# Modulation rows of a decoder layer: summed over partitions by chains of accumulating DMAs instead of matmuls, with loads and norm factors rearranged around them

## The chip, the cores and the metric

The kernel runs on one core of a Trainium2 chip. The metric is the device time of one execution in microseconds (us), the median of several runs. The core has five engines with an instruction list each: TensorE (PE) multiplies matrices and writes to PSUM; VectorE (DVE) and ScalarE (ACT) compute element by element; GpSimd (POOL) does the same more slowly; SyncE (SP) only issues DMAs. Each engine takes its list in order, and waits for others on semaphores. DMAs are issued by SP, ACT and POOL.

## The reference

One decoder layer on 512 tokens of width 1024 in float32:

```python
mod = silu(c) @ w_ada + b_ada                        # (1, 6 * 1024)
shift1, scale1, gate1, shift2, scale2, gate2 = split(mod, 6)
h = rmsnorm(x, norm1_g) * (1 + scale1) + shift1
qa, ka, va, qd, kd, vd, ga, gd = split(h @ w_in)
out_a = sliding_window_attention(qa, ka, va)         # 8 heads, window 128, sinks, ALiBi
out_d = diff_attention(qd, kd, vd)                   # 4 heads, two softmax maps, per-head rmsnorm
merged = sigmoid(ga) * (out_a @ w_branch_swa) + sigmoid(gd) * (out_d @ w_branch_diff)
x = x + gate1 * (merged @ w_out)
h2 = rmsnorm(x, norm2_g) * (1 + scale2) + shift2
a, g = split(h2 @ w_up)                              # 2 * 2816 columns
x = x + gate2 * ((gelu(causal_conv3(a)) * g) @ w_down)
out = rmsnorm(x, final_g)
```

## The kernel before

Every product is made of three matmuls on values split into a high and a low part (`mm3`, lines 122 to 124; `split`, lines 118 and 119: ScalarE casts the high part, VectorE subtracts it to get the low part). The stages follow each other along PE's list:

- **0 to 62 us**: statistics of x, shift1 and scale1 from `w_ada`, the first projection (L385).
- **62 to 308 us, the attention stage**: one long list that the program writes out by hand for PE (`manual_schedule`, L530). Its steps are the scores, softmaxes, transposes and values of four pairs of sliding-window heads (`swa_*`) and of 16 blocks of differential attention (`diff_*`; 4 heads h, 4 query blocks n each). Between them `fill(n)` puts n ticks of plain projections: a tick is one `k` step of three 512-column matmuls of the current unit. Units (weight columns of w_in, or a branch projection) stand in the list `units`; `prefetch` keeps two of them loaded. Buffers for raw weights come from one ring of four (`raw_tile`, L107).
- **308 to 345 us**: the output projection with `gate1` folded into `w_out` (`load_rows`, L1109), `oc`.
- **345 to 690 us**: the second norm, `w_up` with the convolution (`up`, L1274), then `w_down` (`dc`, L1889) and the final norm. Its weight sums are made by accumulating DMAs on POOL (L1183, L1874).

The order on VectorE, ScalarE, POOL and SP in the attention stage isn't written out: a planner orders ready instructions by priority and its own cost estimates. `high_priority` raises, `issue_after` puts behind a given instruction of the same engine.

**The modulation rows.** shift2, scale2 and both gates (four vectors of 1024, eight half rows of 512) are needed only after attention. The generator `ada_rows` makes them beside it: every `ADA_EVERY` = 8 ticks (L561) it loads 256 rows x 512 columns of `w_ada` (`ada_load`, L839), and VectorE multiplies by silu(c) and adds into `ac`, 128 partitions x 512 (`arow`, L861 and L863). Four loads make one half row, which still has to be summed over the 128 partitions. `ada_spread` does that on PE with a matrix of ones:

```python
    nc.tensor.matmul(
        pr[gs], ones[:, gs], ac[:, g * P : (g + 1) * P], start=True, stop=True, tile_position=(0, 32 * g)
    )
```

ScalarE copies the result out (L885), and POOL stores 2 KB of it to `mod_rows` in DRAM (L886). `flush("row")` or `after(ADA_LAG, ...)` says where in PE's list these matmuls stand.

**Who reads `mod_rows`.** `g1b` (gate1, both halves of row 0, L1077, on POOL) multiplies the rows of w_out; `m2` (rows 1 and 2, L1082) is transposed on PE (`pm`, L1086) for the second norm; `g2b` (row 3) is read by the last stage at 468 us.

**The norm factors of differential attention.** `diff_values(h)` multiplies the probabilities with the values. `stats` (flushed in the third block of the next head) takes the sums of squares, and `rstd_m2` makes the factor: POOL raises to a power (L185), VectorE improves it (L193, L195). `turn_norm` (flushed in the first block of the head after that) spreads the factor by four transposes (`rb`, L818) and scales the output.

Of the kernel before, what the change touches and what calls it, by code (L numbers as in the profile page):

```python
# [14 lines left out]
P = 128  # L15
# [11 lines left out]
WB = 3  # L27
HP = 100000
ST = 6
ADA_LAG = 1  # L30
# [6 lines left out]
STAT_LAG = 10  # L37
NORM_LAG = 16
# [16 lines left out]
def kernel(  # L55
# [50 lines left out]
    def raw_tile(shape, name):  # L106
        return wp.tile(shape, F32, tag="raw", bufs=4, name=name)  # L107
# [422 lines left out]
    man.enter_context(tc.manual_schedule(engines={nc.tensor.engine}))  # L530
    units, loaded, later = [], [], []
# [7 lines left out]
    def fill(n):  # L539
        for _ in range(n):  # L540
            if not current:
                prefetch()
                if loaded:
                    wts, run = loaded.pop(0)
                    current.append(run(wts))
                    if tick[0]:
                        prefetch()
# [16 lines left out]
    beside = {"row": [], "sum": [], "norm": [], "turn": []}  # L564
# [153 lines left out]

    def diff_scores(*ss):
# [20 lines left out]
        for s, sps, w in ops:  # L740
# [3 lines left out]
            for m in range(2):  # L744
                st = ap.tile([P, w], F32, tag="st", bufs=ST, name=f"sd{h}_{n}_{m}")
                with tc.high_priority(offset=HP):
                    nc.vector.tensor_tensor_reduce(
                        st, sps[m], ddf[:, 512 - w : 512], 1.0, -3e38, ALU.add, ALU.max, mx[:, m : m + 1]
                    )
# [39 lines left out]
    def diff_values(h):  # L789
# [14 lines left out]
        def stats():  # L804
# [7 lines left out]
            rstd_m2(rs, r2, NT, P, ap)  # L812
            nc.vector.tensor_mul(rs, rs, r0)
# [29 lines left out]
    def ada_rows():  # L843
        todo = [(idx, hf, k) for idx in range(4) for hf in range(2) for k in range(0, KT, 2)]
        r = ada_load(*todo[0])
        yield
        for (idx, hf, k), job in zip(todo, todo[1:] + [None]):
            nxt = ada_load(*job) if job else None
            if k == 0:
                ac = big.tile([P, S], F32, tag=("sq2", "g2b1")[hf], name=f"arow{idx}{hf}")  # L850
            if idx == 0 and hf == 1 and k in ROW_BEHIND:
                hold = tc.issue_after(pairs[sorted(pairs)[ROW_BEHIND[k]]].divided.ins)
            elif tick[0] > ADA_EASY:
                hold = tc.high_priority(offset=HP // 2)
# [9 lines left out]
            if k == KT - 2:  # L864
                row = lambda idx=idx, hf=hf, ac=ac: ada_spread(idx, hf, ac)
                if group_ahead:
                    beside["row"].append(row)
                else:
                    after(ADA_LAG, row)
            r = nxt  # L870
            yield

    spread = []


    def ada_spread(idx, hf, ac):
        pr = tbank(f"pr{idx}{hf}", (P, P))
        for g in range(4):
            gs = slice(32 * g, 32 * g + 32)
            nc.tensor.matmul(  # L880
                pr[gs], ones[:, gs], ac[:, g * P : (g + 1) * P], start=True, stop=True, tile_position=(0, 32 * g)
            )
        row = big.tile([P, P], F32, tag="g2b0", name=f"row{idx}{hf}")
        with tc.high_priority(offset=HP):
            spread.append(nc.scalar.copy(row, pr))  # L885
        nc.gpsimd.dma_start(  # L886
# [1058 lines left out]
```

## Time and profile before

| | us |
|---|---|
| median of 3 runs (lowest, highest) | 692.67 (692.59, 693.79) |
| the profiled execution | 691.85 |
| its span, first to last instruction | 689.8 |
| PE busy in the span | 680.0 |
| DVE busy | 565.5 |
| ACT busy | 383.7 |
| POOL busy | 82.0 |
| granted TensorE clock | 0.997 |

The page of the profile gives the busy time of each engine, the span in 40 slices, DMA queues, the chain of work that ended last, the costliest groups of instructions, and the DMA issues with their time to landing. Further views list who waited for whom, the timeline of an engine, the instructions of a line or a tile, and busy times by windows. L12 is line 12 of the kernel; a releaser stands behind "<-".

### The profile page before, as it was taken

What the parts mean: (1) busy time and instruction counts of PE and PEld (TensorE: products, weight loads), DVE (VectorE), ACT (ScalarE), POOL (GpSimd) and SP (SyncE); (2) the same over time, 40 slices, a digit from 0 to 9 for tenths busy, and PEclk for the clock granted to TensorE, in tenths of its full rate; (3) what the DMA queues carried; (4) which work ended last, traced back from release to release, by engine and by line L of the source; (5) the groups of instructions that cost most, each with busy time, mean ns of one, the idle gap of its engine ahead of it and who ended that gap; (6) DMA issues with size and microseconds to landing.
All of it is one profiled execution on the core that took longest, in us unless ns stands there. A gap on an engine that the chain in (4) does not pass through costs nothing. (4 is left out here: it accounts for less than half of the span.)

```text
span 689.8 us, 11249 instructions
## 1 busy us (share of the span) xinstructions
PE 680.0 (99%) x4203; PEld 592.7 (86%) x4203; DVE 565.5 (82%) x1073; ACT 383.7 (56%) x686; POOL 82.0 (12%) x100
## 2 busy tenths in 40 slices
PE   8999999999999999999999999999999999999995
PEld 5887777788888888888899999999999999888884
DVE  5898987987885666673689988888888999979997
ACT  7676666546543323332477656655555666656665
POOL 3000000000001100000030101112120002540300
PEclk9999999999999999999999999999999999999998
DMA  9985454552555575239635897777888648997903
GB/s 309 350 237 180 140 158 135 166 166 67 153 153 184 185 226 171 91 113 315 214 65 120 179 212 191 173 165 218 193 229 215 154 155 203 197 197 196 167 1 122
DMA packets 115926, 121.81 MB, mean 177 GB/s; under 512 B 4447, under 2 KB 93344, under 8 KB 115872
## 3 DMA queue, kind: packets, MB, share of 16 engines
q1 hardware_dynamic: 96958, 95.09, 43.9%
q0 software_dynamic: 18720, 25.73, 22.3%
q8 instruction: 33, 0.54, 0.3%
q10 hardware_dynamic: 194, 0.28, 0.1%
q14 instruction: 21, 0.17, 0.1%
HBM read 118.97 MB, written 2.11 MB: 176 GB/s over the span
## 5 line engine op out<-in xcount | busy, mean ns | idle before, releaser
L1274 PE MATMUL up<-t,m_whi 128*128 128x256 f32 x512 | 93.1, 283 | 0.0
L1274 PEld LDWEIGHTS up<-t,m_whi 128*128 128x128 f32 x512 | 79.9, 192 | 0.0
L1274 PE MATMUL up<-t,m_wlo 128*128 128x256 f32 x256 | 72.4, 283 | 0.0
L1274 PE MATMUL up<-bh,p_whi 128*128 128x256 f32 x232 | 65.7, 283 | 0.0
L1274 PE MATMUL up<-bl,p_whi 128*128 128x256 f32 x232 | 65.7, 283 | 0.0
L1274 PE MATMUL up<-bh,p_wlo 128*128 128x256 f32 x232 | 65.7, 283 | 0.0
L863 DVE SCALAR_TENSOR_TENSOR arow<-ra,cs,arow 128x512 f32<-128x512 f32 x56 | 42.0, 749 | 18.9 <-DMA ra<-in_w_ada_dram 18.2
L1274 PEld LDWEIGHTS up<-t,m_wlo 128*128 128x128 f32 x256 | 49.2, 192 | 0.0
L1274 PEld LDWEIGHTS up<-bh,p_whi 128*128 128x128 f32 x232 | 44.5, 192 | 0.0
L1274 PEld LDWEIGHTS up<-bl,p_whi 128*128 128x128 f32 x232 | 44.5, 192 | 0.0
L1274 PEld LDWEIGHTS up<-bh,p_wlo 128*128 128x128 f32 x232 | 44.5, 192 | 0.0
L1183 POOL DMA_DIRECT2D s<-in_w_up_dram x21 | 27.0, 1360 | 138.6 <-DMA s<-in_w_up_dram 69.3
L1211 ACT CAST m_whi<-s 128x1024 fp32r<-128x1024 f32 x31 | 32.5, 1047 | 11.1 <-DVE s L1205 7.7
L1215 DVE TENSOR_TENSOR m_wlo<-s,m_whi 128x1024 fp32r<-128x1024 f32 x31 | 37.8, 1218 | 0.0
L1274 PE MATMUL up<-t,p_whi 128*128 128x256 f32 x176 | 32.2, 283 | 0.0
L886 POOL DMA_DIRECT2D mod_rows<-row x8 | 4.9, 612 | 203.4 <-ACT row L885 203.4
L1274 PEld LDWEIGHTS up<-t,p_whi 128*128 128x128 f32 x176 | 27.5, 192 | 0.0
L1281 ACT ACTIVATE gT<-a,cv 128x512 f32<-128x512 f32 x22 | 17.7, 813 | 16.9 <-DVE a L1316 15.8
L185 POOL TENSOR_TENSOR r<-ms,mhalf 128x1 f32<-128x1 f32 (+1 forms) x16 | 12.7, 792 | 120.7 <-DVE ms L183 73.1
L1211 ACT CAST p_whi<-wa 128x1024 fp32r<-128x1024 f32 x18 | 18.8, 1042 | 12.6 <-PE up L1274 12.6
L1215 DVE TENSOR_TENSOR p_wlo<-wa,p_whi 128x1024 fp32r<-128x1024 f32 x18 | 22.0, 1222 | 3.8 <-ACT p_whi L1211 3.2
L1274 PE MATMUL up<-t,p_wlo 128*128 128x256 f32 x88 | 24.9, 283 | 0.0
(491 smaller groups left out, 2063.2 us busy)
## 6 DMA issues: line engine op xcount, KB each, us to landing
ra<-in_w_ada_dram SPq DMA_DIRECT2D x32, 512.0 KB, 4.1
wa<-in_w_up_dram SPq DMA_DIRECT2D x22, 512.0 KB, 4.1
s<-in_w_up_dram SPq DMA_DIRECT2D x21, 512.0 KB, 4.6
s<-in_w_up_dram POOLq DMA_DIRECT2D x21, 512.0 KB, 7.3
adaw<-in_w_ada_dram SPq DMA_DIRECT2D x12, 512.0 KB, 7.3
w<-in_w_in_dram SPq DMA_DIRECT2D x12, 512.0 KB, 4.5
a<-in_w_up_dram SPq DMA_DIRECT2D x11, 512.0 KB, 4.6
b<-in_w_down_dram SPq DMA_DIRECT2D x10, 512.0 KB, 4.6
```

The lines of the kernel that those rows point to most:

```text
L185: nc.gpsimd.tensor_tensor(r0, ms, mhalf[:, :n], ALU.pow)
L863: nc.vector.scalar_tensor_tensor(ac, r[:, a], cc, ac, ALU.mult, ALU.add)
L886: nc.gpsimd.dma_start(mod_rows[idx, hf * S : (hf + 1) * S].rearrange("(g n) -> g n", g=4), row[0:P:32])
L1183: nc.gpsimd.dma_start(dst, upblock(*blk), accum_op=ALU.add)
L1211: nc.scalar.copy(W[J, name][0], R[J, SRC[name]])
L1215: nc.vector.tensor_sub(lo, R[J, SRC[name]], hi.bitcast(F32))
L1274: nc.tensor.matmul(o[u], w[:, k, cu], b[:, k], start=name in ("p1", "m5", "p2") and k == 0 and x == 0, stop=k == 3 and x == 2, skip_group_ ...
L1281: nc.scalar.activation(grow(j), av[J][:, u], AF.Identity, bias=cv[:, 66 + j : 67 + j], scale=cv[:, 44 + j : 45 + j])
```

## The change

- `ada_spread` is gone. `ada_sum` issues, on POOL, seven DMAs that add the upper half of the remaining partitions of `ac` to the lower half (64, 32, 16, 8, 4, 2, 1 partitions of 2 KB), and one that stores partition 0 to `mod_rows`. It is called as soon as the last multiply of the half row is traced; `ac` takes turns in three buffers instead of two.
- The ring of raw buffers has six instead of four; `ada_rows` loads two jobs ahead instead of one, so each multiply is traced 8 ticks later than before; its high priority is dropped. The scratch for DMA descriptors is set to 8192 bytes.
- All units are listed at the start, and `due` counts how many may run, so that `prefetch` can load across the ends of groups. SP's order in the attention stage is that of the program.
- The norm factor is made in two parts: `stats` starts it (the power on POOL), and `end` finishes it after the row maxima of the next scores, one block later; `turn_norm` stands two ticks into the second block of the head after, instead of in the first. For the last head `end` comes 3 ticks after `stats`.
- The broadcasts of `g1b` and its bias, and two constant parts of `m2`, are issued by SP instead of POOL; the two VectorE instructions on `g1b` stand behind the second merge.

```diff
--- before.py
+++ after.py
@@ -25,9 +25,10 @@
 SWA_PAIRS = 4
 DIFF_HEADS = 4
 WB = 3
+RAW = 6
+ADA_AHEAD = 2
 HP = 100000
 ST = 6
-ADA_LAG = 1
 ADA_EVERY = 8
 ADA_EASY = 20
 
@@ -35,6 +36,7 @@
 ADA_START = 4
 V_LAG = 13
 STAT_LAG = 10
+END_LAG = 3
 NORM_LAG = 16
 SWA_FILL = (2, 2, 5, 2, 2, 2, 2, 3)
 DIFF_FILL = (3, 2, 4, 2)
@@ -104,7 +106,7 @@
         return bank("v", 1, [P, S], name)
 
     def raw_tile(shape, name):
-        return wp.tile(shape, F32, tag="raw", bufs=4, name=name)
+        return wp.tile(shape, F32, tag="raw", bufs=RAW, name=name)
 
     splits = []
 
@@ -527,8 +529,8 @@
             mm3(o[:, sl], wh[:, k], wl[:, k], rh[:, k, sl], rl[:, k, sl], k == 0, k == KT - 1)
 
     man = ExitStack()
-    man.enter_context(tc.manual_schedule(engines={nc.tensor.engine}))
-    units, loaded, later = [], [], []
+    man.enter_context(tc.manual_schedule(engines={nc.tensor.engine, nc.sync.engine}))
+    units, loaded, later, due = [], [], [], [0]
     current, tick = [], [0]
 
     def prefetch():
@@ -540,7 +542,8 @@
         for _ in range(n):
             if not current:
                 prefetch()
-                if loaded:
+                if loaded and due[0]:
+                    due[0] -= 1
                     wts, run = loaded.pop(0)
                     current.append(run(wts))
                     if tick[0]:
@@ -561,7 +564,7 @@
             if tick[0] >= ADA_START and tick[0] % ADA_EVERY == 0:
                 next(ada, None)
 
-    beside = {"row": [], "sum": [], "norm": [], "turn": []}
+    beside = {"sum": [], "end": [], "norm": [], "turn": []}
 
     def after(n, fn):
         later.append([n, fn])
@@ -716,6 +719,8 @@
     AW = 384
 
 
+    maxima = []
+
     def diff_scores(*ss):
         ops = []
         for s in ss:
@@ -744,9 +749,9 @@
             for m in range(2):
                 st = ap.tile([P, w], F32, tag="st", bufs=ST, name=f"sd{h}_{n}_{m}")
                 with tc.high_priority(offset=HP):
-                    nc.vector.tensor_tensor_reduce(
+                    maxima.append(nc.vector.tensor_tensor_reduce(
                         st, sps[m], ddf[:, 512 - w : 512], 1.0, -3e38, ALU.add, ALU.max, mx[:, m : m + 1]
-                    )
+                    ))
                 pm.append(st)
             scored[s] = mx, pm
 
@@ -809,8 +814,16 @@
             nc.vector.reciprocal(r0, sums[h][:, 0])
             nc.vector.tensor_mul(r2, r0, r0)
             nc.vector.tensor_mul(r2, r2, pss)
-            rstd_m2(rs, r2, NT, P, ap)
-            nc.vector.tensor_mul(rs, rs, r0)
+            half = rstd_start(r2, NT, P, ap)
+
+            def end():
+                rstd_end(rs, *half, NT, ap)
+                nc.vector.tensor_mul(rs, rs, r0)
+
+            if h < 3:
+                beside["end"].append(end)
+            else:
+                after(END_LAG, end)
 
             def turn_norm():
                 rb = tbank(f"rb{h}")
@@ -842,16 +855,18 @@
 
     def ada_rows():
         todo = [(idx, hf, k) for idx in range(4) for hf in range(2) for k in range(0, KT, 2)]
-        r = ada_load(*todo[0])
-        yield
-        for (idx, hf, k), job in zip(todo, todo[1:] + [None]):
-            nxt = ada_load(*job) if job else None
+        ready = []
+        for job in todo[:ADA_AHEAD]:
+            ready.append(ada_load(*job))
+            yield
+        for (idx, hf, k), job in zip(todo, todo[ADA_AHEAD:] + [None] * ADA_AHEAD):
+            r = ready.pop(0)
+            if job:
+                ready.append(ada_load(*job))
             if k == 0:
-                ac = big.tile([P, S], F32, tag=("sq2", "g2b1")[hf], name=f"arow{idx}{hf}")
+                ac = big.tile([P, S], F32, tag=("sq2", "g2b1", "g2b0")[(2 * idx + hf) % 3], name=f"arow{idx}{hf}")
             if idx == 0 and hf == 1 and k in ROW_BEHIND:
                 hold = tc.issue_after(pairs[sorted(pairs)[ROW_BEHIND[k]]].divided.ins)
-            elif tick[0] > ADA_EASY:
-                hold = tc.high_priority(offset=HP // 2)
             else:
                 hold = tc.issue_after(pairs[0].first.ins)
             with hold:
@@ -862,30 +877,15 @@
                     else:
                         nc.vector.scalar_tensor_tensor(ac, r[:, a], cc, ac, ALU.mult, ALU.add)
             if k == KT - 2:
-                row = lambda idx=idx, hf=hf, ac=ac: ada_spread(idx, hf, ac)
-                if group_ahead:
-                    beside["row"].append(row)
-                else:
-                    after(ADA_LAG, row)
-            r = nxt
+                ada_sum(idx, hf, ac)
             yield
 
-    spread = []
-
-
-    def ada_spread(idx, hf, ac):
-        pr = tbank(f"pr{idx}{hf}", (P, P))
-        for g in range(4):
-            gs = slice(32 * g, 32 * g + 32)
-            nc.tensor.matmul(
-                pr[gs], ones[:, gs], ac[:, g * P : (g + 1) * P], start=True, stop=True, tile_position=(0, 32 * g)
-            )
-        row = big.tile([P, P], F32, tag="g2b0", name=f"row{idx}{hf}")
-        with tc.high_priority(offset=HP):
-            spread.append(nc.scalar.copy(row, pr))
-        nc.gpsimd.dma_start(
-            mod_rows[idx, hf * S : (hf + 1) * S].rearrange("(g n) -> g n", g=4), row[0:P:32]
-        )
+    def ada_sum(idx, hf, ac):
+        n = P // 2
+        while n:
+            nc.gpsimd.dma_start(ac[0:n], ac[n : 2 * n], accum_op=ALU.add)
+            n //= 2
+        nc.gpsimd.dma_start(mod_rows[idx : idx + 1, hf * S : (hf + 1) * S], ac[0:1])
 
 
     pair_w = {}
@@ -905,8 +905,7 @@
                         wba[256 * a : 256 * a + 256, j * P : (j + 2) * P].rearrange("(i p) n -> p i n", p=64),
                     )
 
-                with tc.issue_after(spread[-1].ins) if j == 0 else ExitStack():
-                    pair_w["a"] = split_pair(r, [P, 4, 2 * P], f"wba{j}")
+                pair_w["a"] = split_pair(r, [P, 4, 2 * P], f"wba{j}")
             return pair_w["a"]
 
         def branch(wts):
@@ -918,11 +917,18 @@
         units.append((lambda: load_cols(win, COL_GA + j * P, f"wga{j}"), gate))
         units.append((load, branch))
 
-    group_ahead, sums = [1], {}
+    sums = {}
     pairs, firsts, scored, probs, aTs = {}, {}, {}, {}, {}
     ada = ada_rows()
-    add_head(0)
-    add_head(1)
+    for h in range(2):
+        add_head(h)
+    for j in range(2):
+        add_gate_a(j)
+    for h in range(2, DIFF_HEADS):
+        add_head(h)
+    for j in range(2, KT):
+        add_gate_a(j)
+    due[0] = 6
     with tc.issue_after(last_mod.ins):
         prefetch()
     fill(SWA_FILL[0])
@@ -940,7 +946,6 @@
         more = i + 1 < SWA_PAIRS
         fill(SWA_FILL[3])
         if more:
-            flush("row")
             swa_scores(i + 1, range(NT))
         swa_transpose(i, 0)
         fill(SWA_FILL[4])
@@ -953,58 +958,51 @@
                 swa_softmax(i + 1)
         fill(SWA_FILL[6])
         if i < 2:
-            flush("row")
             swa_values(i)
         fill(SWA_FILL[7])
-    while units or loaded or current:
+    while due[0] or current:
         fill(1)
-    flush("row")
     swa_values(2)
     swa_values(3)
 
     outd = [big.tile([P, 4, S], F32R, tag=f"kv{x}", name=f"outd{x}") for x in "AB"]
     ta = big.tile([P, KT, S], F32, tag="qa", name="ta")
-    for j in range(2):
-        add_gate_a(j)
+    due[0] += 4
     diff_scores(0, 1)
     diff_softmax(0, 1)
     fill(DIFF_FILL[0])
     for s in range(4 * DIFF_HEADS):
         h, n = divmod(s, NT)
         if s in (4, 8):
-            add_head(h + 1)
+            due[0] += 3
         elif s == 12:
-            add_gate_a(2)
-            add_gate_a(3)
+            due[0] += 4
         ahead = s == 1
         fill(DIFF_FILL[1] - ahead)
         nxt = (s + 1, s + 2) if n % 2 and s < 15 else ()
         if nxt:
-            flush("row")
             diff_scores(*nxt)
+        if n == 3:
+            with tc.issue_after(maxima[-1].ins):
+                flush("end")
         if n == 1:
             diff_transpose(s)
-        fill(DIFF_FILL[2] + ahead)
+            fill(2)
+            flush("norm")
+        fill(DIFF_FILL[2] + ahead - 2 * (n == 1))
         if n == 2:
             flush("sum")
-        elif n == 0:
-            flush("norm")
         if n != 1:
             diff_transpose(s)
-        if s == 13:
-            group_ahead.clear()
-        elif s > 13:
-            flush("row")
         diff_softmax(*nxt)
         if n == 0 and h:
             diff_values(h - 1)
             fill(DIFF_FILL[3])
-    for j in range(4, KT):
-        add_gate_a(j)
-    fill(4)
+    due[0] += 2 * (KT - 4)
+    fill(6)
     flush("norm")
     diff_values(DIFF_HEADS - 1)
-    while units or loaded or current:
+    while due[0] or current:
         fill(1)
     at.close()
 
@@ -1030,6 +1028,8 @@
             nc.scalar.activation(tds[j], o, AF.Tanh, scale=0.5)
 
         units.append((lambda: load_cols(win, COL_GD + j * P, f"wgd{j}"), gate))
+
+    merged = []
 
     def add_merge(j):
         def load():
@@ -1049,7 +1049,7 @@
             td = tds[j]
             nc.vector.scalar_tensor_tensor(td, td, 1.0, o, ALU.add, ALU.mult)
             nc.vector.tensor_add(td, td, ta[:, j])
-            split(mgh[j], mgl[j], td)
+            merged.append(split(mgh[j], mgl[j], td))
 
         units.append((load, branch))
 
@@ -1058,7 +1058,8 @@
         if j:
             add_merge(j - 1)
     add_merge(KT - 1)
-    while units or loaded or current or later:
+    due[0] += len(units)
+    while due[0] or current or later:
         fill(1)
     for _ in ada:
         fill(1)
@@ -1067,21 +1068,22 @@
     man.close()
 
 
-    def brow(dst, src):
-        nc.gpsimd.dma_start(dst, src.partition_broadcast(P))
+    def brow(dst, src, q=nc.gpsimd):
+        q.dma_start(dst, src.partition_broadcast(P))
 
     TAIL = 3
     xnp = [gpart(i, [P, 2, D], f"xn{i}") for i in range(2)]
     g1b = gpart(4, [P, D], "g1b")
     g1bias = xnp[0][:, 0]
-    brow(g1b, mod_rows[0])
-    brow(g1bias, b_ada[0, 2 * D : 3 * D])
-    nc.vector.tensor_add(g1b, g1b, g1bias)
-    nc.vector.tensor_scalar_mul(g1b, g1b, 0.5)
+    brow(g1b, mod_rows[0], nc.sync)
+    brow(g1bias, b_ada[0, 2 * D : 3 * D], nc.sync)
+    with tc.issue_after(merged[1][1].ins):
+        nc.vector.tensor_add(g1b, g1b, g1bias)
+        nc.vector.tensor_scalar_mul(g1b, g1b, 0.5)
     m2 = bp.tile([40, P], F32, name="m2")
+    nc.sync.dma_start(m2[16:32, :], b_ada[0, 3 * D : 5 * D].rearrange("(a p) -> a p", p=P))
+    nc.sync.dma_start(m2[32:40, :], norm2_g[0].rearrange("(a p) -> a p", p=P))
     nc.gpsimd.dma_start(m2[0:16, :], mod_rows[1:3].rearrange("r (a p) -> (r a) p", p=P))
-    nc.gpsimd.dma_start(m2[16:32, :], b_ada[0, 3 * D : 5 * D].rearrange("(a p) -> a p", p=P))
-    nc.gpsimd.dma_start(m2[32:40, :], norm2_g[0].rearrange("(a p) -> a p", p=P))
     pm2 = tbank("pm2", (P, 40))
     nc.tensor.transpose(pm2, m2, ident[:40, :40])
     c2 = bp.tile([P, 40], F32, name="c2")
@@ -1929,7 +1931,7 @@
     import concourse.bacc as _bacc
     from concourse.bass_utils import run_bass_kernel_spmd as _run
 
-    nc = _bacc.Bacc("TRN2", target_bir_lowering=False, num_devices=1)
+    nc = _bacc.Bacc("TRN2", target_bir_lowering=False, num_devices=1, dynamic_dma_scratch_size=8192)
     arrays, args = {}, []
     for name in _INS:
         a = _np.ascontiguousarray(inputs[name])
```

## The prediction

> **What bounds the kernel now.** I read the page first (sections 1 and 4), then the waits of PE alone, then a table of windows, then the timeline of PE around the instructions that the change removes.
>
> ```profile
> PE 680.0 (99%) x4203; PEld 592.7 (86%) x4203; DVE 565.5 (82%) x1073; ACT 383.7 (56%) x686; POOL 82.0 (12%) x100
> PE up L1274 32%; PE dc L1889 15%; PE th L1369 1%; ACT sqo L1346 0%; PE oc L1334 0%; PE oc L1330 0%; PE oc L1331 0%; POOL r L185 0%; ACT early L1411 0%; DVE xn L1359 0%; ACT x L1815 0%; POOLq L1941 0%; ACT sqe L1800 0%; DVE rt L191 0%; DVE x L1795 0%
> PE a L174 <- POOL ones L133: 1.0, 1, 1.0
> PE tp L656 <- DVE st L644: 0.4, 1, 0.4
> PE xt L408 <- DVE xn L403: 0.4, 1, 0.4
> 115.00:205.00 90.00, 90.00 (x511) 72.92 (x510) 74.82 (x211) 48.44 (x116) 4.92 (x6) 1.00 0.49 141
> 205.00:285.00 80.00, 80.00 (x387) 64.91 (x387) 50.17 (x67) 24.92 (x35) 6.01 (x10) 1.00 0.59 183
> ```
>
> TensorE (PE) is busy for 680.0 of 689.8 us. Its waits on other engines come to about 2 us, and only one of them (0.4 us, on line 644) lies in the attention stage that the change rewrites. The two windows (columns: busy time of PE, weight loads, VectorE, ScalarE, GpSimd, then granted clock, DMA share and GB/s) show PE without a gap at full clock from 115 to 285 us, and VectorE with 15 us free in 90 and 30 us free in 80. So a microsecond taken off PE's list here is a microsecond of the kernel, as long as nothing else comes late; all other engines matter only where they make PE wait. After 361 us the chain is PE alone (up, dc), so what is won before it is kept.
>
> **Removed: the spreading matmuls.** Eight times PE sums a row over partitions (L880).
>
> ```profile
> L880 PE MATMUL pr<-arow,ones x64: 272/285/298, 107.6 to 282.3; 128*32 128x128 f32 x64
> L885 ACT COPY row<-pr x8: 265/267/285, 108.3 to 282.6; 128x128 f32<-128x128 f32 x8
> 281.79 0.39 PE L124 MATMUL pgd<-hThA,wgd_l 128*128 128x512 f32 x1
> 282.11 0.43 PE L880 MATMUL pr<-arow,ones 128*32 128x128 f32 x8
> 282.46 0.50 PE L122 MATMUL pgd<-hThA,wgd_h 128*128 128x512 f32 x1
> 282.80 0.39 PE L123 MATMUL pgd<-hTlA,wgd_h 128*128 128x512 f32 x1
> 283.03 0.39 PE L124 MATMUL pgd<-hThA,wgd_l 128*128 128x512 f32 x1
> ```
>
> Starts, not durations, tell the cost, since matmuls overlap. An ordinary step is 283.03 - 282.80 = 0.23 us. From 281.79 to 282.46 are 0.67 us where 0.23 would do, so one spread costs 0.44 us; the matmul after it takes 0.34 instead of 0.23 until the next start, 0.1 more. Eight times 0.44 is 3.5 us; the 0.1 I count for the four spreads among gate matmuls, 0.4. Sum: -3.9 us on the path. The eight copies on ScalarE (8 x 0.27 us of an engine that is half idle) and the PSUM buffers that they held go too; they bound nothing, so 0.
>
> **Added: chains of DMAs on GpSimd (POOL).** Each row is now halved seven times by accumulating DMAs (64, 32, ... 1 partitions of 2 KB), then stored: 8 links instead of one, each reading what the link before wrote, so each waits for the landing, and POOL waits with it, in order.
>
> ```profile
> L886 POOL DMA_DIRECT2D mod_rows<-row x8: 541/603/768, 108.9 to 283.2; - x8
> DMA to landing us min/median/max: 1.6/3.1/4.7
> 238.51 0.60 POOL L886 DMA_DIRECT2D mod_rows<-row  x1 [4.63 <-ACT row L885]
> 240.45 0.50 POOL L1082 DMA_DIRECT2D m<-mod_rows  x1 [1.34 <-DMA mod_rows<-row]
> s<-in_w_up_dram POOLq DMA_DIRECT2D x21, 512.0 KB, 7.3
> DMA to landing us min/median/max: 6.0/7.3/11.3
> 77.83 0.75 DVE L863 SCALAR_TENSOR_TENSOR arow<-ra,cs,arow 128x512 f32<-128x512 f32 x1
> 261.97 0.74 DVE L863 SCALAR_TENSOR_TENSOR arow<-ra,cs,arow 128x512 f32<-128x512 f32 x1
> 312.05 1.39 POOL L1183 DMA_DIRECT2D s_t<-in_w_up_dram  x1 [28.34 <-DVE c L1092]
> 327.54 1.05 ACT L118 CAST m5w<-s_t 128x1024 fp32r<-128x1024 f32 x1 [1.74 <-DVE wo L1109]
> L1086 PE MATMUL pm<-ident,m x1: 252/252/252, 307.9 to 307.9; 40*128 40x40 f32 x1
> ```
>
> No row shows a small accumulate inside SBUF, so I bound a link. The one dependent pair of the trace is 240.45 - 238.51 = 1.94 us, 0.3 more than the shortest landing (1.6). At the longest (4.7) a link is 5.0, at the median (3.1) 3.4. The accumulates carry 254 KB per row; a 512 KB accumulate lands in 7.3, so (7.3 - 3.1)/512 per KB adds 2.1 us per row. A row then takes 17.6 us (8 x 1.94 + 2.1), 29.3 at the median, 42.1 at the worst.
>
> When must it be done? The first row's sum ends at 78.6 and the last at 262.7 (the two L863 rows). Loading two jobs ahead moves each multiply 8 ticks back; 32 ticks are one row, (283.2 - 108.9)/7 = 24.9 us, so 8 are 6 us: 84 and 269. The rows come 26 us apart. The first customer is the transpose of m2 on PE (307.9), which needs six rows; the next is POOL's own accumulate at 312.05 (s_t), whose landing, 11.3 us at the longest of that line, comes at 323.4, some 4 us before the ScalarE cast at 327.54 takes it. Less the 3.9 that PE is now ahead, the last chain must end by 312. From 84 that is 228 us for 64 links, 3.56 us a link. I take 3.5, 28 us a row, a little below the median because sources and targets no longer lie in DRAM (an estimate; nothing shows it); the last chain then ends at 308, and six rows at 252. So the chains hide, with little to spare: 0, and +24 if a link is 4.0 (first rival).
>
> [...]
>
> **Moved: the norm factors.** POOL also computes the power for each head (L185), now queued between links.
>
> ```profile
> 153.45 1.04 POOL L185 TENSOR_TENSOR r<-ms,mhalf 128x4 f32<-128x4 f32 x1 [21.04 <-DVE dr L809]
> 178.64 1.03 POOL L185 TENSOR_TENSOR r<-ms,mhalf 128x4 f32<-128x4 f32 x1 [10.73 <-DVE ms L181]
> DVE rt L193 <- POOL r L185: 4.4, 4, 1.2
> DVE arow L863 <- DMA ra<-in_w_ada_dram: 18.2, 15, 2.8
> ```
>
> A head is 25.2 us (178.64 - 153.45), a block 6.3. Before, VectorE waited at once for the power (up to 1.2 us). Now the start stands in the third block, the end after the row maxima of the next scores, a block later, and the transposes that use it two blocks after that. So the power has 6.3 - 1.0 = 5.3 us of cover, one or two links. What is queued behind the waiting VectorE instruction is everything in order: evacuations, softmax, low parts of weights; PE has shown that it can take a VectorE wait of 2.8 us (the longest on L863) without one of its own. I take +0.6 us for all four heads together, between -0.4 (the wait on L644 disappears as well) and +13 (second rival). The spread itself is moved by one block, but still ahead of the branch matmuls: 0.
>
> **Loads: six buffers, two ahead, one fixed order on SP.** VectorE's 18.2 us of waiting for modulation weights should mostly go. PE does not wait for that now, so it is worth 0. The weights keep a cover of their own:
>
> ```profile
> w<-in_w_in_dram SPq DMA_DIRECT2D x12, 512.0 KB, 4.5
> L118 ACT CAST w_h<-w 128x1024 fp32r<-128x1024 f32 x12 | 12.5, 1049 | 5.4 <-PE pw L123 3.2 <-PE pA L123 1.3 <-ACT pT L658 0.6
> L119 DVE TENSOR_TENSOR w_l<-w,w_h 128x1024 fp32r<-128x1024 f32 x12 | 14.6, 1219 | 0.7 <-ACT w_h L118 0.7
> ```
>
> Landing, cast and low part take 4.5 + 1.05 + 1.22 = 6.8 us, and they are asked for two units ahead, 2 x 24 matmuls x 0.23 = 11 us before use. In SP's fixed order a modulation load that waits for its buffer holds the weights behind it; from 4 us of that on PE would wait, and two more buffers speak against it: 0. The bias loads that leave POOL for SP come behind the last weight load, and the row that needs them is late enough:
>
> ```profile
> 266.44 0.37 SPq L1038 DMA_DIRECT2D wbd<-in_w_branch_diff_dram  x1
> L1109 DVE TENSOR_TENSOR wo<-wo,g1b x8: 1217/1222/1226, 274.9 to 326.3; 128x1024 f32<-128x1024 f32 x8
> ```
>
> g1b asked for at 267 lands by about 272, before the product at 274.9, and the first output matmul comes only after 308. The cover here is over 20 us; 0. Multiplies of modulation rows lose their priority, which at worst holds buffers longer: 0 to +1, in the range. The smaller descriptor scratch shows in no row; 0.
>
> **Sum.** -3.9 + 0.6 = -3.3 us on the profiled execution's 691.85 us (span 689.8 and 2 us around it): 688.5. The median of the runs before (692.67) lies 0.8 above that execution, so I forecast 689.3 for the median. About 0.2%, 1.4 us, is what a measurement of this kernel can tell from no change.
>
> **Rivals.**
> First, the POOL queue becomes the bound (slower). It decides from 3.56 us a link, and the median link with its bytes is 29.3/8 = 3.66, so this is close. If a link takes 4.0 us, the last chain ends at 84 + 64 x 4.0 = 340, and s_t comes 28 us late. ScalarE stands at the cast of m5w with the last two casts of w_out behind it, and PE, after about 4 us of products that it still has, waits for those: 689 + 24 = 713. At 3.75 it is 324, 12 us late: 697. At 3.65 it is 318: 691, still faster. For it: loads now run evenly, so fewer links meet a quiet DMA. Against: the landing of 1.6 and the pair of 1.94 where no load is near. [...] Chance 0.17.
>
> Second, VectorE stands behind the power (slower). If the power sits four links late in POOL's order, that is 14 us against 5.3 of cover: VectorE stops for 8.7, PE absorbs 2.8, and three heads cost 3 x 5.9 = 18, in all 707. At three links it is 10.5, so 5.2 less 2.8, three times 2.4 = 7: 696. It decides where the power comes more than 8 us late. For it: rows 26 us apart with chains of 28 leave POOL no pause. Against: it needs only one link to end before it goes. Chance 0.16.
>
> Third, the time is won and lost again (no change): PE reaches the output projection 3.9 us earlier and waits there for weights or for the norm of the first rows. For: the norm lines (L1346, L185, L191, L1359) stand in the chain of section 4. Against: the norm starts from PE's own results and moves with it. 692.7. Chance 0.07.
>
> **Numbers.** The forecast, with everything from a small loss of VectorE time to none, has 0.60. Faster by over 0.2%: 0.60. Same: 0.07. Slower: 0.17 + 0.16 = 0.33. The likeliest case alone runs from 687.8 (-3.9 - 0.4 - 0.5 more from VectorE's freed waits) to 691.2 (+2 of VectorE waiting). The range reaches up over the milder halves of both rivals: 687.5 to 699; about 0.15 lies above it and 0.04 below.
>
> **What would show it.** Right: no L880 in PE's list, PE steps of 0.23 through those places, PE's waits still about 2 us, transposes of m2 near 304 instead of 307.9, the last chain's store on POOL before 312, and the span 3 to 4 us shorter. Wrong: waits "DVE rt <- POOL r" of several us and PE waits on DVE behind them (second rival), or the s_t accumulate well after 312 and ScalarE standing at m5w (first). Links under 2.5 us would say that I feared too much.

## The result and the profile after

The changed kernel takes 696.28 us (median of 11 runs, 694.73 to 700.29) against 693.25 us (11 runs, 691.37 to 694.57) of the kernel before on the same chip: a ratio of 1.0058, 95% interval 1.0045 to 1.007. It is slower by 3 us; 689.3 was forecast. The profiled executions have spans of 694.3 and 689.8 us.

The engines' busy times, section 1 of the page after (line numbers have moved by a few lines; the links are now L886, the power L187, its use L195):

```profile
PE 678.1 (98%) x4139; PEld 592.2 (85%) x4139; DVE 564.2 (81%) x1073; ACT 381.7 (55%) x678; POOL 123.8 (18%) x152
```

The 64 spreading matmuls are gone (4203 before), and PE is still not done earlier. The windows of the attention stage, before and then after (columns as in the prediction), and the five microseconds behind the longest stall of after:

```profile
62.00:345.00 283.00, 282.59 (x1517) 228.77 (x1516) 206.37 (x472) 130.28 (x284) 13.65 (x19) 1.00 0.55 166
```

```profile
62.00:345.00 283.00, 276.62 (x1431) 224.36 (x1430) 201.36 (x463) 125.11 (x270) 55.24 (x70) 0.99 0.59 172
...
164.00:169.00 5.00, 4.97 (x19) 4.38 (x20) 2.30 (x5) 1.45 (x4) 1.18 (x2) 0.66 0.64 169
```

PE stands idle for 6.4 us of these 283, where it stood for 0.4: 6.0 more. Just after the stall the granted clock is 0.66 on average over 5 us, and 0.50 in shorter windows from 166 to 168; that makes 3.4 us at half clock, or 1.7 us lost. From this go the 3.9 us of matmuls that are no longer there: 6.0 + 1.7 - 3.9 = 3.8 of the 4.5 us between the two spans. The other 0.7 lie ahead of the stage: PE is busy for 57.3 of the first 60 us instead of 58.1. I do not count that as an effect of the change: in the profiles of the first four runs below this figure lies anywhere from 56.3 (no links) to 58.6 (chains alone).

What PE waits for, from the view of the waits of PE alone (total us, times, longest), and three rows of all waits:

```profile
PE td L789 <- DVE dls L775: 3.1, 3, 2.4
PE pgd L124 <- DVE ta L915: 1.3, 1, 1.3
PE td L789 <- DVE sd L777: 1.3, 1, 1.3
...
POOL arow L886 <- DMA arow<-arow: 129.0, 48, 5.9
DVE arow L878 <- DMA ra<-in_w_ada_dram: 21.4, 14, 3.9
DVE rt L195 <- POOL r L187: 8.0, 2, 5.1
```

PE waits for VectorE, VectorE for POOL (twice, 8.0 us in all), and POOL for its own links. One of the two places, read from POOL, VectorE and PE in the timeline:

```profile
152.89 0.88 POOL L886 DMA_DIRECT2D arow<-arow  x1 [3.20 <-DMA arow<-arow]
157.81 0.77 POOL L886 DMA_DIRECT2D arow<-arow  x1 [4.04 <-DMA arow<-arow]
158.34 1.31 POOL L187 TENSOR_TENSOR r<-ms,mhalf 128x4 f32<-128x4 f32 x1
```

```profile
154.22 0.16 DVE L183 TENSOR_SCALAR ms<-dr 128x4 f32<-128x4 f32 x1
...
159.68 0.16 DVE L195 TENSOR_TENSOR rt<-r 128x4 f32<-128x4 f32 x1 [2.88 <-POOL r L187]
...
159.83 0.74 DVE L878 SCALAR_TENSOR_TENSOR arow<-ra,cs,arow 128x512 f32<-128x512 f32 x1
...
160.60 0.75 DVE L878 SCALAR_TENSOR_TENSOR arow<-ra,cs,arow 128x512 f32<-128x512 f32 x1
...
161.35 1.22 DVE L121 TENSOR_TENSOR w_l<-w,w_h 128x1024 fp32r<-128x1024 f32 x1
...
163.08 0.15 DVE L775 RECIPROCAL dls<-dls 128x1 f32<-128x1 f32 x1
```

```profile
161.25 0.39 PE L126 MATMUL pq<-hThA,w_l 128*128 128x512 f32 x1
164.03 0.30 PE L789 MATMUL td<-ident,sd 128*128 128x128 f32 x1 [2.39 <-DVE dls L775]
```

The power's input `ms` is ready at 154.4. POOL has issued a link at 152.89 and its next instruction is another link, which stands until the first has landed and is issued at 157.81. The power, queued behind it, ends at 159.65. VectorE reached its use of the power at 156.80 and waited 2.88 us; behind it in order stand two row multiplies, a low part, an evacuation and only then the reciprocal that the next block's transposes on PE need. So PE stands. The second place is head 3:

```profile
224.58 0.16 DVE L183 TENSOR_SCALAR ms<-dr 128x4 f32<-128x4 f32 x1
229.89 0.16 DVE L195 TENSOR_TENSOR rt<-r 128x4 f32<-128x4 f32 x1 [5.15 <-POOL r L187]
```

There VectorE has nothing at all between the input and the use, and stands for 5.15 us; a stall of PE (1.3 us, on L915) follows some 20 us later. The chains themselves end in time:

```profile
L886 POOL DMA_DIRECT2D arow<-arow x56: 750/790/1138, 75.0 to 287.1; - x56
289.19 0.52 POOL L888 DMA_DIRECT2D mod_rows<-arow  x1 [1.32 <-DMA arow<-arow]
L1088 PE MATMUL pm<-ident,m x1: 252/252/252, 312.7 to 312.7; 40*128 40x40 f32 x1
```

The 56 links and 8 stores take from 75.0 to 289.2, 3.4 us each with the pauses between rows; the transposes of m2 come at 312.7, 4.8 us later than before.

### The profile page after: what moved, and what is told of

Read it like the earlier page. It is cut to its first block, busy times and chain, and to the rows that moved or that the text cites. A ratio compares the mean times of both kernels' runs of the same rounds, so it can differ in the third digit from the quotient of the medians.

```text
span 694.3 us, 11164 instructions
## 1 busy us (share of the span) xinstructions
PE 678.1 (98%) x4139; PEld 592.2 (85%) x4139; DVE 564.2 (81%) x1073; ACT 381.7 (55%) x678; POOL 123.8 (18%) x152
## 4 chain that ended last, share of the span: by engine, by line
PE 74%; DMA 16%; DVE 5%; issue 3%; POOL 1%; ACT 0%; SPq 0%; POOLq 0%; DVEq 0%; ACTq 0%
PE up L1276 32%; PE dc L1891 15%; DMA arow<-arow 13%; PE a L387 5%; PE oc L1332 2%; PE oc L1333 2%; PE oc L1336 2%; DMA ra<-in_w_ada_dram 2%; PE pgd L124 2%; PE pgd L126 2%; PE pgd L125 2%; DVE arow L878 1%; DMA adaw<-in_w_ada_dram 1%; PE pB L124 1%; PE pB L126 1%
## 5 line engine op out<-in xcount | busy, mean ns | idle before, releaser
L886 POOL DMA_DIRECT2D arow<-arow x56 | 45.1, 814 | 196.8 <-DMA arow<-arow 129.0
L878 DVE SCALAR_TENSOR_TENSOR arow<-ra,cs,arow 128x512 f32<-128x512 f32 x56 | 41.8, 747 | 21.9 <-DMA ra<-in_w_ada_dram 21.4
L187 POOL TENSOR_TENSOR r<-ms,mhalf 128x1 f32<-128x1 f32 (+1 forms) x16 | 13.4, 842 | 80.2 <-DVE ms L185 73.3
L772 ACT ACTIVATE sd<-sd,dmx 128x128 f32<-128x128 f32 (+3 forms) x32 | 17.7, 555 | 14.9 <-DVE dmx L762 14.8
```

The lines of the kernel that those rows point to most:

```text
L772: exp = nc.scalar.activation(pm[m], pm[m], AF.Exp, bias=mx[:, m : m + 1], scale=slope, accum_out=ls)
L878: nc.vector.scalar_tensor_tensor(ac, r[:, a], cc, ac, ALU.mult, ALU.add)
L886: nc.gpsimd.dma_start(ac[0:n], ac[n : 2 * n], accum_op=ALU.add)
```

## The experiments

Theory A: links make the -1/2 power on POOL late, and VectorE, in order, stands behind it with work that PE needs; late modulation loads add to that. Rival B: the links cost through their transfers, which make other DMAs late. Rival C: the edits around the links (loads, SP's order, the dropped priority) cost, not the links. The kernel before took 692.5 to 692.7 us beside these runs; a gain on the changed kernel is given as the difference to its 696.28 us, and by the ratios it is up to 0.6 us larger. The base of each edit stands behind its name.

**No links** (after):

```
     def ada_sum(idx, hf, ac):
-        n = P // 2
-        while n:
-            nc.gpsimd.dma_start(ac[0:n], ac[n : 2 * n], accum_op=ALU.add)
-            n //= 2
         nc.gpsimd.dma_start(mod_rows[...], ac[0:1])
```

> The changed kernel with the seven accumulating DMAs of each row left out (POOL only stores partition 0, so the sum over partitions is not computed). Theory A (PE's 3.6 us are really saved and are overpaid in three places: the power of the norm factor queued on POOL between links, and VectorE standing at multiplies whose load has not landed, partly because the broadcasts moved to SP): the wait of VectorE for the power (8.0 us, longest 5.1) falls to about 2, PE's stall at 161 us and the half clock behind it go, so the time falls by 3 to 4 us against the changed kernel, to about the time of before or 0.5 us under it (ratio 0.999 to 1.002); the stalls near 118, 189 and 251 us stay. Rival B (the links' traffic slows all loads): all four stalls go, ratio about 0.994. Rival C (the fixed order on SP and the lost priority are the whole loss): nothing goes, ratio 1.005.

Measured: 690.14 us, ratio 0.9961 [0.9948, 0.9973]. Everything else in the change costs nothing; the links cost 696.28 - 690.14 = 6.1 us. C falls. The number lies between those of A and B, so it does not tell these two apart. Of the stalls that A had expected to stay, the one near 118 us does (1.0 us); those near 189 and 251 shrink to 0.3 us and to nothing.

**g1b back on POOL** (after):

```
-    brow(g1b, mod_rows[0], nc.sync)
-    brow(g1bias, b_ada[0, 2 * D : 3 * D], nc.sync)
+    brow(g1b, mod_rows[0])
+    brow(g1bias, b_ada[0, 2 * D : 3 * D])
```

> The changed kernel with the two 512 KB broadcasts of g1b and its bias issued by POOL again. Theory A: the modulation load that stood behind them on SP lands some 2 to 3 us earlier, VectorE's wait of 3.95 us at 251 us shrinks under 2 and PE's 1.5 us stall there goes: 1.5 us less than the changed kernel (ratio to before about 1.003 to 1.004), the rest unchanged. Rivals B and C: B no change (ratio 1.006); C 1 to 2 us less.

Measured: 702.66 us, ratio 1.0144 [1.0118, 1.0169], 6.4 us above the changed kernel and outside what A gave. PE's waits and two windows of its profile:

```profile
PE td L789 <- DVE dls L775: 5.0, 3, 4.4
PE pgd L124 <- DVE ta L915: 4.6, 1, 4.6
...
167.00:175.00 8.00, 8.00 (x29) 6.77 (x29) 3.08 (x6) 2.99 (x5) 2.38 (x3) 0.63 0.55 151
260.00:268.00 8.00, 7.28 (x23) 5.83 (x24) 5.02 (x7) 0.00 (x0) 1.58 (x2) 0.68 0.70 210
```

Both stalls are there, the second now 4.6 us, and behind each the granted clock is 0.63 and 0.68 on average over 8 us (5 to 6 us of it at half, an estimate from these averages). The second follows a modulation load whose multiply starts 8.2 us after the load's issue (5.1 in the changed kernel), beside the bias broadcast from POOL. It is 3.3 us longer than in the changed kernel and has 2.6 us of lost clock behind it, which is most of the 6.4 us that SP's taking these two loads is worth here. The first stall is longer by 2 us although the lists of all engines are the same up to there, and this execution, the slowest of the five, took 3.6 us more than their median. How late the power comes hangs on how long the links ahead of it took: the one whose landing it had to await was issued 0.3 us after the power's input was ready, in the changed kernel 1.5 us before.

**Chains alone** (before; three row buffers, links in place of the spreading; the hold of one weight split behind the old copy goes too):

```
-    row = lambda idx=idx, hf=hf, ac=ac: ada_spread(idx, hf, ac)
-    ...
+    ada_sum(idx, hf, ac)
```

> The kernel before with the chains of accumulating DMAs in place of the spreading matmuls and nothing else of the change (the factor is finished at once, not a block later). Theory A: PE saves 3.6 us, but every head's power now stands behind links and VectorE waits for it at once, 3 to 6 us in each of four heads with PE absorbing up to 2.8 of each: net 0 to 8 us slower than before (ratio 1.000 to 1.012), with waits of VectorE for POOL of over 8 us in all. Rival B: PE waits on late loads instead, ratio about 1.005, no longer wait for POOL. Rival C: 3.6 us faster, ratio 0.995.

Measured: 704.8 us, ratio 1.018 [1.0158, 1.0202]. From all waits and from PE's:

```profile
DVE rt L193 <- POOL r L185: 12.4, 3, 6.8
PE rb L818 <- DVE drs L813: 6.8, 1, 6.8
```

The time lies above what A gave (up to 1.012). Used at once, as the kernel before did, the power holds VectorE for 12.4 us and PE for 6.8 in one piece. Ending the norm factors later and the other edits are worth 8.5 us to the links; they are a repair of what the links do, and not a full one.

**No spreading** (before; POOL stores one partition of the row, no matmuls, no copy, and no hold of a weight split behind that copy):

```
     def ada_spread(idx, hf, ac):
-        pr = tbank(f"pr{idx}{hf}", (P, P))
-        ...
-            spread.append(nc.scalar.copy(row, pr))
-        nc.gpsimd.dma_start(mod_rows[...], row[0:P:32])
+        nc.gpsimd.dma_start(mod_rows[...], ac[0:1])
```

> The kernel before with the spreading matmuls and the copies behind them left out, POOL storing partition 0 (the sum over partitions is not computed). All theories: the work that the change takes off PE measured by itself, 8 x 0.45 = 3.6 us, up to 4.0 with the slower first matmul behind each: ratio 0.9945, unless the freed time comes back as a wait later, then 0.997 to 1.000.

Measured: 692.77 us, ratio 1.000 [0.9991, 1.001]. The 3.9 us of PE work go, and nothing comes of it:

```profile
62.00:345.00 283.00, 278.77 (x1448) 226.93 (x1447) 204.76 (x472) 127.70 (x275) 13.82 (x19) 1.00 0.55 166
...
PE tp L656 <- ACT qkv L490: 2.0, 1, 2.0
PE rb L818 <- DVE drs L813: 0.8, 1, 0.8
```

PE's idle time in the stage rises from 0.4 to 4.2 us, by about what was freed. But the edit takes away more than work. Before, the first multiply of the next half row waits on VectorE until `pr` has read its buffer, and stands behind the softmax; without the spreading the planner puts it, with its wait for a load, in front. The kernel before, then this run:

```profile
102.14 1.08 DVE L644 TENSOR_SCALAR st<-st,lsum 128x128 f32<-128x128 f32 x4
...
108.13 0.48 DVE L861 TENSOR_SCALAR arow<-ra,cs 128x512 f32<-128x512 f32 x1 [2.26 <-PE pr L880]
```

```profile
102.65 0.49 DVE L861 TENSOR_SCALAR arow<-ra,cs 128x512 f32<-128x512 f32 x1 [1.25 <-DMA ra<-in_w_ada_dram]
...
104.25 1.08 DVE L644 TENSOR_SCALAR st<-st,lsum 128x128 f32<-128x128 f32 x4
...
104.68 1.14 PE L656 MATMUL tp<-ident,st 128*128 128x128 f32 x7 [2.01 <-ACT qkv L490]
```

The division of the softmax (L644), which these transposes on PE read, comes 2.1 us later, and PE waits 2.0 us, ahead of the place of the first matmul that was taken out (107.6). The view names the cast that ended last; in the kernel before the transposes ran ahead of that cast, so I read the wait as one for L644. With 0.7 us more at the next division (L644, from 107.46), behind two further multiplies, this makes 2.7 of the 3.8 us. So the run shows that the freed time did not become time of the kernel. That the engines which feed PE had nothing in hand, with their lists unchanged, it does not show.

**Spreading back** (after; the summing as before, two row buffers):

```
-    ada_sum(idx, hf, ac)
+    row = lambda idx=idx, hf=hf, ac=ac: ada_spread(idx, hf, ac)
+    ...
```

> The changed kernel with only the summing put back to the spreading over PE and the copy on ScalarE (loads, norm factors, g1b and the dropped priority stay changed). Theory A (the links on POOL delay the -1/2 power, and VectorE stands behind it): without links VectorE waits for POOL in the heads for under 0.5 us; the time is that of the run without links plus at most the 3.6 us of PE work, 690.1 to 693.7, ratio 0.996 to 1.002 to the kernel before. Rival C (the other edits, loads and dropped priority, are what costs): 695 to 698 stays.

Measured: 691.61 us, ratio 0.9986 [0.9976, 0.9995], as A said for the time. VectorE still waited 2.3 us for the power (under 0.5 was expected), without a stall of PE. The rest of the change gains 1.0 us without links: C falls a second time.

**No power** (after; the head's power on POOL replaced by a reciprocal on VectorE):

```
-        nc.gpsimd.tensor_tensor(r0, ms, mhalf[:, :n], ALU.pow)
+        nc.vector.reciprocal(r0, ms)
```

> The changed kernel with all links, but with the -1/2 power of the four heads replaced by a reciprocal on VectorE (0.16 us each; the norm factor is then another number), so that nothing that VectorE waits for stands in POOL's queue behind a link. Theory A: the stall of 2.5 us near 161 us and the half clock behind it go, 3.5 to 5 us of the 6.2 us that the links cost come back: 691 to 693, ratio 0.997 to 1.001. Rival B (the links cost through their transfers, which make other loads late): 695 to 696.5.

Measured: 690.62 us, ratio 0.9967 [0.9955, 0.9979], 0.4 us under what A gave. All 56 links run, with all their transfers, and 5.7 of their 6.1 us are gone. This tells A from B: what is left for the transfers is 0.5 us, within the intervals of the two runs.

**g1b behind the last load** (after):

```
+    with tc.issue_after(last_ra[-1].ins):       # last modulation load on SP
         brow(g1b, mod_rows[0], nc.sync)
         brow(g1bias, b_ada[0, 2 * D : 3 * D], nc.sync)
```

> The changed kernel with the broadcast of g1b and of its bias on SP issued behind the last modulation load instead of ahead of it. Theory A: VectorE's wait of 3.95 us for the modulation load near 250 us falls below 1.5 us and PE's stall of 1.47 us there goes; the rest stays: 694.5 to 695.2. Rival B (the load is late from the links' own transfers): the wait stays over 3 us and the time within 0.3 us of the changed kernel's 696.3.

Measured: 697.04 us, ratio 1.0061 [1.0045, 1.0077], no better than the changed kernel. From its timeline, the load on SP and the multiply on VectorE:

```profile
247.51 0.37 SPq L854 DMA_DIRECT2D ra<-in_w_ada_dram  x1
...
251.90 0.75 DVE L880 SCALAR_TENSOR_TENSOR arow<-ra,cs,arow 128x512 f32<-128x512 f32 x1 [3.27 <-DMA ra<-in_w_ada_dram]
```

The load lands within 4.4 us of its issue, as such loads do in the changed kernel (median 4.2); VectorE comes to it only 1.1 us after the issue. This part of A falls: g1b's place on SP is not the cause. The run without the power, with the same order on VectorE, shows where it comes from:

```profile
243.48 0.75 DVE L881 SCALAR_TENSOR_TENSOR arow<-ra,cs,arow 128x512 f32<-128x512 f32 x1 [2.28 <-DMA ra<-in_w_ada_dram]
```

There the load, which also takes 4.4 us, is issued 2.3 us before VectorE comes to it, and no matmul stops. So the stall near 251 us is a later effect of the waits for the power; the next run, in which head 3's is left, still has 0.9 us of it.

**Ends of heads 0 to 2 behind the softmax** (after):

```
-        if n == 3:
-            with tc.issue_after(maxima[-1].ins):
-                flush("end")
         ...
         diff_softmax(*nxt)
+        if n == 3:
+            with tc.issue_after(spreads[-1].ins):   # last product of the softmax on VectorE
+                flush("end")
```

> The changed kernel with the norm factors of heads 0 to 2 ended behind the softmax of the blocks in work instead of behind their row maxima (some 6 us later on VectorE, ahead of the norm's transposes as before; the same instructions). Theory A: the wait for the power (2.9 us near 159 us) is under 0.5 us, and nothing that PE needs is behind it: 691.5 to 693.5, ratio 0.998 to 1.001. Rival B (transfers): 695.5 to 696.5. Rival D (the norm's own transposes on PE now wait for the factor): a new PE wait for drs, 696 to 699.

Measured: 692.67 us, ratio 1.0002 [0.9989, 1.0015]. 3.6 us of the changed kernel's time are won by moving twelve small instructions down VectorE's list. Of the two waits for the power one is left, head 3's:

```profile
DVE rt L195 <- POOL r L187: 6.1, 1, 6.1
PE pgd L124 <- DVE ta L916: 0.9, 1, 0.9
PE pA L124 <- DVE ta L916: 0.9, 1, 0.9
```

**Head 3's end alone** (after; behind the next gate product on VectorE, the norm's transposes four steps later):

```
-                after(END_LAG, end)
+                after(END_LAG, end_behind)     # end() within tc.issue_after(gated[-1].ins)
-END_LAG = 3, NORM_LAG = 16
+END_LAG = 9, NORM_LAG = 20
```

> The changed kernel with head 3's end alone moved behind the gate product (heads 0 to 2 end behind their row maxima as in the changed kernel). Theory A: head 0's wait near 159 us and the stall of 2.5 us there stay, head 3's wait is under 0.5 us: 2 us better than the changed kernel, 694 to 695; with the 3.6 us of the other three heads this adds up to the run without the power. Rival B: 695.5 to 697.

Measured: 694.16 us, ratio 1.0027 [1.0015, 1.004]: 2.1 us won. 3.6 + 2.1 = 5.7 us, what the run without the power won. Head 0's stall is still there, the stalls of PE that followed head 3's wait are not:

```profile
PE td L789 <- DVE dls L775: 2.9, 3, 2.5
...
DVE rt L195 <- POOL r L187: 4.2, 2, 3.0
```

The other of these two waits, 1.2 us, is head 3's (under 0.5 was expected) and stops no matmul. The late load near 250 us is still there too; what PE needs, `ta`, now stands ahead of its multiply on VectorE:

```profile
248.18 0.69 DVE L920 SCALAR_TENSOR_TENSOR ta<-ta,pA 128x512 f32<-128x512 f32 x1
252.98 0.75 DVE L883 SCALAR_TENSOR_TENSOR arow<-ra,cs,arow 128x512 f32<-128x512 f32 x1 [4.11 <-DMA ra<-in_w_ada_dram]
```

How much of the 2.1 us is this order, and how much the shorter wait for the power, this run does not tell.

**Both ends late** (after, the two edits above together):

> The changed kernel with the ends of heads 0 to 2 behind the softmax, and head 3's behind the next gate product on VectorE with its norm's transposes four steps later on PE. Theory A: both waits of VectorE for the power are under 0.5 us, and with head 3's wait (6.1 us with only the first three moved) goes what follows it, late modulation loads and two PE stalls of 1.0 us: 690.0 to 691.5, ratio 0.996 to 0.999, faster than before by what the run without the power had. Rival B (transfers): no better than the 692.7 of moving heads 0 to 2 alone. Rival D: a PE wait for the factor of head 3 takes the gain back.

Measured: 690.51 us, ratio 0.9969 [0.9954, 0.9983]. Faster than the kernel before by 2 us, with all links in place. VectorE no longer waits for the power in any head. The windows of the stage:

```profile
62.00:345.00 283.00, 280.87 (x1457) 228.45 (x1457) 206.16 (x476) 129.00 (x279) 56.55 (x72) 1.00 0.59 173
```

PE's idle time is 2.1 us, and its clock is not halved any more.

**And a multiply behind** (both ends late, and the first multiplies of the fourth row behind the first block's softmax):

```
+            elif (idx, hf, k) == (1, 1, 0):
+                hold = tc.issue_after(spreads[0].ins)
```

> As the run with both ends late, and the first two multiplies of the fourth row stand behind the first block's softmax on VectorE instead of ahead of it (they wait for their load there). Theory A with the even loads as a second, smaller cost: PE's stall of 1.4 us near 118 us falls below 0.5 us, 1 us less than both ends late: 689.0 to 690.5. Rival: the stall moves to the next block, same time as both ends late.

Measured: 689.40 us, ratio 0.9961 [0.9948, 0.9973]. This is the time that was expected, and four of the five executions are shorter than the shortest with both ends late. The interval overlaps the last one, though, and PE's waits do not bear out the expected reason:

```profile
PE td L790 <- DVE sd L777: 0.7, 1, 0.7
PE td L790 <- DVE qkv L493: 0.4, 1, 0.4
PE td L790 <- DVE dls L775: 0.4, 2, 0.2
```

One wait of 1.0 us (both ends late) has become two of 0.7 and 0.4. The multiplies wait for their load wherever they stand. Whether it is faster stays open.

**Both ends late, spreading back** (the same ends, the summing on PE and ScalarE):

> Both ends late, as in the run that beat the kernel before, but with the summing on PE and ScalarE as before instead of the links on POOL: what the links bring once nothing waits for the power. If the prediction's 3.9 us of PE work are all worth their time, this is 3.5 to 3.9 us above the run with links (690.5), 694.0 to 694.4; if PE's freed time is mostly taken up by the waits for the softmax, as in the run without the spreading (0 us gained there), it is within 1.5 us, 690.5 to 692.

Measured: 691.36 us, ratio 0.9988 [0.9974, 1.0001]; its stage:

```profile
62.00:345.00 283.00, 282.97 (x1519) 229.05 (x1518) 205.48 (x474) 129.72 (x284) 12.44 (x15) 1.00 0.54 166
```

With no stall behind the power, links instead of matmuls come out 691.36 - 690.51 = 0.85 us better, which is not clear of noise (their intervals overlap). PE has 0.03 us of idle time with the spreading and 2.1 with the links: over half of the freed 3.9 us come back as waits, and the two largest (1.0 and 0.8 us) again stand behind modulation multiplies on VectorE.

## Why the prediction was wrong, step by step

- **The sign, and the step that failed: "I take +0.6 us" for the power on POOL.** It cost 5.7 us (no power, both ends late), so 696.28, though inside the stated range, lies on the other side of the kernel before. Two figures under it were wrong. The cover was given as 5.3 us for each head; VectorE came to its use 2.4 us after the input in head 0 (156.80 against 154.38), and at once in head 3, whose end hangs on a lag of three ticks and which I had not costed apart. And PE was said to take 2.8 us of VectorE waiting, from L863; a wait of 2.88 us in front of the softmax gave a stall of 2.39. How long a wait may be is a matter of what stands behind it in that place. The 1.7 us of half clock behind that stall stood in no term.
- **Second rival.** Its mechanism is what happened: chance 0.16, price 696 to 707. Its threshold was off: it was to decide from a power more than 8 us late; the power came 5.3 and 5.1 us after its input in heads 0 and 3, behind the landing of a single link, and that was enough. The sentence against it, that it needs only one link to end, was true and beside the point, since one link could be 4.9 us. That its milder price, 696, is the measured time is luck: it was made of three heads that stall PE, each with the power 10.5 us late.
- **-3.9 us of PE work.** Right in size (680.0 to 676.1 us of busy time with both ends late), wrong in worth: 0 where it was taken out of the kernel before, 0.85 (not clear of noise) with the late ends, and 691.61 - 690.14 = 1.5 between spreading back and no links, clear of their intervals. "A microsecond taken off PE's list here is a microsecond of the kernel" held only under its proviso, that nothing else comes late: without the spreading, which had held their buffer, modulation multiplies came ahead of the softmax on VectorE, and PE waited there. In sum the runs give 692.6 - 1.0 (the rest of the change) - 1.5 (the matmuls) + 6.1 (the links) = 696.2.
- **First rival, the POOL queue.** Fell. The link that I took (3.5) was measured at 3.4, the last store came at 289.2, ahead of the 312 that I set. A row takes 27 us with the pauses, where I took 28. That a link lies a little below the median because sources and targets are not in DRAM was my estimate, which no run tests; the links landed in 3.0 us at the median (1.8 to 6.5), the stores of before in 3.1.
- **Loads, "0".** The time was right (the rest of the change without links is 1.0 us faster than before), the reading was not: VectorE's wait for modulation loads was to go mostly, and it is 21.4 us instead of 18.2.
- **g1b on SP, "0".** Right: putting it behind the last load changes nothing. That it would cost 6.4 us on POOL was not in my list.
- **Third rival, won and lost again.** It has a part in the truth, at another place: what PE gains is lost in the attention stage, not at the output projection.

## What to carry to other kernels

Each link here that waited for the one before it held POOL's queue until that one had landed (48 waits, 129.0 us in all, the longest 5.9), so ask of every chain what else lives in that queue, who waits for that, and how far ahead of its use it is issued; here it was a power of 1.3 us in a chain of 3.4 us links. If a short result passes through such a queue, put its use far behind in the consumer's list, behind all that the bottleneck needs: moving sixteen small instructions was worth 5.8 us. And before counting work taken off a full engine as time, remove that work alone, and look at what else has moved: here it gained nothing, and most of what was freed came back as waits behind VectorE instructions that nothing held back any more.

## What the runs showed of the hardware

Some stalls of PE cost more than their length here, since the granted clock fell behind them. In the changed kernel a stall of 2.4 us was followed by 3.4 us at half clock, 1.7 us more; in the run with g1b on POOL the clock was 0.63 and 0.68 in the 8 us windows shown behind stalls of 4.4 and 4.6 us. Behind a stall of 2.5 us in the run with head 3's end alone PE was slow too: its 128x384 matmuls (`od`) at 167.65 and 167.94 took 0.50 and 0.52 us, where the same two take 0.33 and 0.34 at full clock in the changed kernel (164.87 and 165.04). A stall of 2.7 us in the run with g1b behind the last load, which ended at 165.30, had full clock behind it:

```profile
165.00:170.00 5.00, 4.70 (x25) 4.14 (x26) 2.75 (x8) 2.73 (x5) 1.02 (x2) 1.00 0.67 182
```

So the length of the stall does not decide it here: slow PE followed 2.4 us in one run and 2.5 in another, and did not follow 2.7 in a third. What does decide it, no run here shows.
